# Decay exponents in float32r, and ungrouped projections as one 512-column product with the parts added at eviction

## The chip, the cores and the metric

The kernel runs on one core of a Trainium2 chip. The metric is the time of one execution on the device, in microseconds (us); 2571.78 us is the median of three runs of the kernel before. TensorE multiplies, VectorE, ScalarE and GpSimd do element-wise work, and SyncE's queue issues all the transfers that this text speaks of. PEld is TensorE's loading of weights.

## The reference

Two layers of a decoder trunk of width 2048 over 256 positions. Each layer has eight gated DeltaNet heads and sixteen query heads of sliding-window attention side by side, then a SwiGLU feed-forward part; both halves are modulated by six vectors that come from c.

```
h      = rms_norm(x) * (1 + scale) + shift
qkv, z, b, a, aq, ak, av = split(h @ w_in)        # the projections
q, k, v = silu(causal_conv4(qkv))                  # 4 taps, per channel
g      = -exp(a_log) * softplus(a + dt_bias);  beta = sigmoid(b)
gc     = cumsum(g) in chunks of 64
decay  = exp(where(causal, gc[c] - gc[s], -inf))
lower  = strict(beta * k k^T * decay) + 1;  t_inv = inverse(lower)
o      = delta rule with t_inv, decay, q, k, v;  o = norm(o) * silu(z)
x     += gate * ([o, attention] @ w_out);  x += gate * swiglu(rms_norm(x) ...)
```

## The kernel before

All values are transposed: 128 channels on the partitions, 256 positions along the free side. An activation tile `act` of h holds two halves side by side, the rounded value in float32r (hi) and the rest (lo), 128x512 together. A weight tile is split the same way by ScalarE (`wh`) and VectorE or GpSimd (`wl`). A *block* is the product of one 128x128 weight tile with one activation tile, summed into PSUM over the 16 tiles of h. `mm3` does it as three products of 256 columns (wh with hi, wh with lo, wl with hi) into one 256-column sum. `mm2` does it as two: wh with both halves at once (512 columns, two sums side by side) and wl with hi (256 columns, onto the first). `gemm` uses `mm3`; `gemm_two` and `gemm_pair` use `mm2`. In the feed-forward part all products are `mm2`.

`JOBS` lists the projections of a layer: `ak`, `av`, `aq` for attention, and `k`, `q`, `v`, `z` per DeltaNet head. `project` starts one and hands its PSUM sum `pm` to the work behind it: `conv_silu` (four taps: one ScalarE operation and three VectorE multiply-adds, all reading `pm`), `gate` (z), `attention` or `kv_heads` (rope). In layer 0 the projections that `EARLY` names are computed in groups while h is still coming in, their parts kept in SBUF and added by `added`. `gemm_quad` does the first four of layer 1. The rest, 14 in layer 0 (v of heads 2 to 7 and all z) and 38 in layer 1, are whole projections of 16 blocks, here called ungrouped.

`scores` forms, per head, the decay exponents: GpSimd multiplies the triangular mask `tri` by g (a w3 buffer), three float32 products with the lower mask `ls` and with ones turn that into sums over stretches of g (`qe`), and ScalarE takes the exponential. With it and the products of k and q, VectorE builds the matrix `B` and the small matrices for the inverse. After four heads, `inverses` inverts their chunks in a batch: eight small transfers (`carry`, L126 in the profile: `qi<-mc`) bring the 16x16 blocks to a shape on which VectorE works, eight more bring the result back (`uc<-ui`), and then masks `U`, transposes with `con` (an identity), and a chain of small products of `W`, `U`, `y`, `yn` and `V` follow. `delta` runs the recurrence of one head. A `v` projection of head h waits in `project`'s loop until the delta rule of head h-2 has got to its middle, and that waits for the inverses: two waits per layer, one per batch. In the rest of this text they are the first and the second inverse of a layer.

Modulation vectors are computed beside all that: tiles `wada` of the modulation matrix, each multiplied with `cs` on TensorE or (`CUSTOM_DVE_ANT_0`, `ISA` in the order of instructions) on VectorE.

The order on each engine is fixed when the kernel is built: `Steps` keeps the pending pieces of work and places one when its engine's planned clock allows, by the prices of `Timed` (a fixed and a per-element part per engine) and a constant of 300 ns from one step to the next; `Weights` places loads (six units ahead, four buffers) and splits. So another operation, or another buffer, changes where later ones are put. On the chip each engine runs its own list in order. All instructions are recorded on line 172.

Of the kernel before, what the change touches and what calls it, by code (L numbers as in the profile page):

```python
# [20 lines left out]
F32 = mybir.dt.float32  # L21
F32R = mybir.dt.float32r
AF = mybir.ActivationFunctionType
ALU = mybir.AluOpType
PSUM = bass.MemoryType.PSUM

D, T, L, H, NH, FT = 2048, 256, 2, 8, 16, 44
# [37 lines left out]

CONST = Cols()
for _n, _w in (
    ("ident", 128), ("triX", 256), ("sel", 8), ("ls", 128), ("amask", 256), ("cos", 256), ("sin", 256),
    ("own", 128), ("id16", 16), ("bm", 8), ("m16", 8),
):  # L70
    CONST.add(_n, _w)
PAR = Cols()
# [25 lines left out]
P_, D_, A_, G_, N_ = "tensor", "vector", "scalar", "gpsimd", None  # L98
# [86 lines left out]
JOIN = 4, 2  # L185


HEADS = {"pm": 3, "psm": 5}, {"w3": 5, "B": 6, "z": 3, "dn": 2, "ry": 2}
FFN = {"pr": 2, "psm": 4}, {"mid": NMID}

START = HEADS[0], {"ry": 1, "wx": 8}

STAGE_TOO = {"ak", "vT", "U", "W", "V", "dy", "av", "junk", "yn", "qi", "ui", "uc", "mc", "hi", "y16", "wy"}


class Build:
# [237 lines left out]
def trunk(tc, xT, bada, c, c_col, par, con, w_in, w_ba, w_ada0, w_ada, w_out, w_gu, w_dn, out):  # L434
    nc = Timed(tc.nc)
    with (
# [3 lines left out]
        b = Build(nc, sb, tc)  # L440
        b.lay(START)
        S = Steps(nc)
        pr = b.t("par", [128, PAR.n])
        cn = b.t("con", [128, CONST.n])
        x = b.t("x", [128, KT, T])
        cs = b.t("cs", [128, D])
        cc = b.t("cc", [128, KT])
        mod = b.t("mod", [128, L, 96])
        def wide(a):
            return CONST.at[a][0]  # L450

        nc.dma(cc, c_col)
        nc.gpsimd.memset(cs[:, 0 : KT * 32 + 32], 0.0)
        nc.dma(mod, bada)
        nc.dma(pr, par)
        nc.dma(cn[:, : wide("ls")], con[:, : wide("ls")])
        x_at = [nc.dma(x[:, lo : lo + 4, :], xT[:, lo : lo + 4, :]) for lo in range(0, KT, 4)]

        def P(name, lo=0, hi=None):
# [3 lines left out]
        def C(name):  # L463
            a, n = CONST.at[name]
            return cn[:, a : a + n]

        ident, triX, ls = C("ident"), C("triX"), C("ls")
        tri, ones = triX[:, 0:128], triX[:, 128:256]
        one = ones[:, 0:1]
        half_c = b.t("halfc", [128, 2, 2])  # L470
        nc.vector.memset(half_c[:, 0, :], 0.5)
# [2 lines left out]
        W = Weights(b)  # L474
# [221 lines left out]
        def pump():  # L696
            while first:
                kind, n = first[0]
                if kind == 0 and ada.room():
                    ada.load()  # L700
                elif kind == 1 and W.room():
                    W.load(n)
                elif kind == 2 and b.free["kq"]:
                    load_ba(0)
                    nc.dma(cn[:, wide("ls") :], con[:, wide("ls") :])
                else:
                    break
                first.pop(0)
            u = W.unit()
            if not first:  # L710
                W.load(u + W.AHEAD + 1)
                ada.loads(u)
            W.split(W.p + W.SPLIT, force=False)
# [25 lines left out]
        def gemm(acts, lo=0, hi=None, tag="pm"):  # L739

            S.grab(b, tag)
            q = b.bank(tag)[:, 0:T]
            into(q, mm3, acts, lo, len(acts) if hi is None else hi)
            return Held(q, lambda: b.give(tag))

        def gemm_two(acts, lo=0, hi=None, tag="pm"):

            S.grab(b, tag)
            q = b.bank(tag)
            into(q, mm2, acts, lo, len(acts) if hi is None else hi)  # L750
            return Held(q, lambda: b.give(tag))
# [233 lines left out]
        def added(q, i, then):  # L985
# [3 lines left out]
            q.drop()  # L989
            yield from then(Held(to, lambda: drop_partial(i)))  # L990

        def betas(l, hs, got):
            while None in hs:
                yield N_
            ws = w_of[l]
            yield from b.take("psm", P_)
            q = b.bank()
            for k in range(KT):
                at = slice(k % 4 * 32, k % 4 * 32 + 32)
                nc.tensor.matmul(  # L1000
                    q[at, :], ws[:, k, :], hs[k].rearrange("p a c -> p (a c)").bitcast(F32), start=k < 4, stop=k >= KT - 4
                )
            b.give("kq")
            yield from b.take("cv", A_)
            w = b.t("cv", [128, T])
            nc.scalar.copy(out=w, in_=q[:, 0:T])
            yield D_
            nc.vector.tensor_tensor(out=w, in0=w, in1=q[:, T:], op=ALU.add)
            b.give("psm")
            yield from b.take("psm", P_)  # L1010
            q = b.bank()
            for tb in range(2):
                nc.tensor.matmul(
                    q[:, tb * 16 : tb * 16 + 16], w[:, tb * 128 : tb * 128 + 128], C("id16"), start=True, stop=True
                )
            b.give("cv")
            yield D_
            ba = b.t("ba", [128, 2, 16], bufs=1)
            nc.vector.tensor_copy(out=ba.rearrange("p a c -> p (a c)"), in_=q[:, 0:32])
            b.give("psm")  # L1020
            yield A_
            beta = b.t("beta", [128, 2, 8], bufs=2)
            nc.scalar.activation(out=beta, in_=ba[:, :, 0:8], func=AF.Tanh, scale=0.5)
            na = b.t("nega", [128, 8], bufs=1)
            nc.scalar.activation(out=na, in_=P(f"a_log{l}"), func=AF.Exp)

            v, u, s, s2, y = (b.t(n, [128, 2, 8], bufs=1) for n in ("sp_v", "sp_u", "sp_s", "sp_s2", "sp_y"))
            yield D_
            for tb in range(2):
                nc.vector.tensor_tensor(out=v[:, tb, :], in0=ba[:, tb, 8:16], in1=P(f"dt{l}"), op=ALU.add)  # L1030
            nc.vector.scalar_tensor_tensor(out=u, in0=v, scalar=-1.0, in1=v, op0=ALU.mult, op1=ALU.max)
            yield A_
            nc.scalar.activation(out=u, in_=u, func=AF.Exp, scale=-1.0)
            yield D_
            nc.vector.tensor_scalar(out=beta, in0=beta, scalar1=0.5, scalar2=0.5, op0=ALU.mult, op1=ALU.add)
            nc.vector.tensor_scalar(out=na, in0=na, scalar1=-1.0, scalar2=None, op0=ALU.mult)
            yield D_
            nc.vector.tensor_scalar(out=s, in0=u, scalar1=2.0, scalar2=None, op0=ALU.add)
            nc.vector.reciprocal(out=s, in_=s)
            nc.vector.tensor_tensor(out=s, in0=s, in1=u, op=ALU.mult)  # L1040
            nc.vector.tensor_tensor(out=s2, in0=s, in1=s, op=ALU.mult)
            nc.vector.tensor_scalar(out=y, in0=s2, scalar1=2.0 / 15, scalar2=2.0 / 13, op0=ALU.mult, op1=ALU.add)
            for n in (11, 9, 7, 5, 3, 1):
                nc.vector.tensor_tensor(out=y, in0=y, in1=s2, op=ALU.mult)
                nc.vector.tensor_scalar(out=y, in0=y, scalar1=2.0 / n, scalar2=None, op0=ALU.add)
                if n in (9, 5):
                    yield D_
            nc.vector.tensor_tensor(out=y, in0=y, in1=s, op=ALU.mult)
            g = b.t("g", [128, 2, 8], bufs=2)
            nc.vector.scalar_tensor_tensor(out=g, in0=v, scalar=0.0, in1=y, op0=ALU.max, op1=ALU.add)  # L1050
            for tb in range(2):
                nc.vector.tensor_tensor(out=g[:, tb, :], in0=g[:, tb, :], in1=na, op=ALU.mult)
            got += [beta, g]

        def rope(q, res):
            yield from b.take("cv", N_)
# [165 lines left out]
        def scores(l, h, st, bt):  # L1222

            while len(st["bg"]) < 2:
                yield N_
            beta, g = st["bg"]
            yield from b.take("w3", G_)
            gt = b.t("w3", [128, 384])
            nc.gpsimd.tensor_tensor(out=gt[:, 0:256], in0=triX, in1=g[:, 0, h : h + 1].to_broadcast([128, 256]), op=ALU.mult)
            nc.gpsimd.tensor_tensor(out=gt[:, 256:384], in0=tri, in1=g[:, 1, h : h + 1].to_broadcast([128, 128]), op=ALU.mult)  # L1230
            yield from b.take("psm", P_)
            qe = b.bank()
            nc.tensor.matmul(qe[:, 0:256], ls, gt[:, 0:256], start=True, stop=False)
            nc.tensor.matmul(qe[:, 128:256], ones, gt[:, 256:384], start=False, stop=True)
            nc.tensor.matmul(qe[:, 256:384], ls, gt[:, 256:384], start=True, stop=True)
            b.give("w3")
            yield from b.take("w3", A_)
            E = b.t("w3", [128, 384])
            nc.scalar.activation(out=E, in_=qe[:, 0:384], func=AF.Exp)
# [16 lines left out]
            g1, g2 = b.bank(), b.bank()  # L1256
# [18 lines left out]
            B = b.t("B", [128, 2, 384])  # L1275
# [317 lines left out]
        for l in range(L):  # L1593
# [7 lines left out]
            def project(kind, h, then, rank=1):  # L1601
                if (kind, h) in four:
                    S.add(then(four[kind, h]), rank)
                elif l == 0 and (kind, h) in EARLY:
                    i = TILES.index((kind, h))
                    S.add(added(gemm(hs, *GROUPS[-1]), i, then), rank)
                else:
                    S.add(then(gemm(hs)), rank)

            def put(q):  # L1610
                kvq.append(q)
# [133 lines left out]
```

## Time and profile before

| | |
|---|---|
| median of three runs | 2571.78 us (2567.96 to 2573.69) |
| the profiled execution | 2571.36 us |
| its span, first to last instruction | 2569.6 us |
| mean granted TensorE clock | 0.980 |
| TensorE busy | 2462.8 us, 96% |
| VectorE, ScalarE, GpSimd busy | 1854.1, 1294.3, 432.7 us |
| read from memory | 603.44 MB, 236 GB/s over the span |

The program's stages lie in the span like this: start and first norm to about 180 us, heads of layer 0 to about 550, its output projection and feed-forward part to about 1375, heads of layer 1 to about 1700, its output projection and feed-forward part to the end. A row of the groups gives engine, operation, output<-inputs, shapes, count, then total busy time and the mean duration of one in ns, then idle time before them and what ended it. A row of the timeline gives start, length, engine, line, operation, with idle time before it and its releaser in brackets.

### The profile page before, as it was taken

How to read it: one execution, taken by the hardware profiler on the slowest of the kernel's cores; microseconds unless marked ns; L12 is line 12 of the kernel's file. 1: busy time of each engine (PE TensorE's matmuls, PEld its weight loads, DVE VectorE, ACT ScalarE, POOL GpSimd, SP SyncE). 2: the span in 40 equal slices, each digit the busy share in tenths (PEclk: the TensorE clock that was granted, in tenths of full speed). 3: DMA queues.
4: the chain of work that ended last, by engine and by line, in shares of the span. 5: the costliest groups of instructions: out<-in, count | busy, mean ns of one | idle time of the engine just before them, and what ended most of it. 6: DMA issues, size and time to landing. Idle time of an engine off the chain costs nothing.

```text
span 2569.6 us, 46036 instructions
## 1 busy us (share of the span) xinstructions
PE 2462.8 (96%) x16878; PEld 2174.5 (85%) x16878; DVE 1854.1 (72%) x3823; ACT 1294.3 (50%) x2760; POOL 432.7 (17%) x389
## 2 busy tenths in 40 slices
PE   6999898988999999999999999899899999999998
PEld 4887786987888888888888899899788888888887
DVE  3758767787667999999987876655877655555665
ACT  4346553535545445555445655454555544555553
POOL 1433232670000000000004333246000000000000
PEclk9999998998999999999999999899999999999999
DMA  9987575776777999999984443346677766555564
GB/s 353 338 302 255 194 244 181 249 272 199 244 245 268 341 354 347 352 345 344 328 299 132 133 131 126 118 161 225 214 253 246 243 187 191 189 183 195 180 185 137
DMA packets 192789, 609.08 MB, mean 237 GB/s; under 512 B 27825, under 2 KB 39217, under 8 KB 192561
## 3 DMA queue, kind: packets, MB, share of 16 engines
q1 hardware_dynamic: 192562, 606.14, 68.9%
q8 instruction: 132, 2.16, 0.3%
q14 instruction: 95, 0.78, 0.1%
HBM read 603.44 MB, written 2.10 MB: 236 GB/s over the span
## 4 chain that ended last, share of the span: by engine, by line
PE 52%; issue 32%; DVE 9%; DMA 3%; ACT 2%; POOL 1%; SPq 1%; DVEq 0%; POOLq 0%; ACTq 0%
PE psm L172 19%; PE pr L172 18%; PE pm L172 15%; DMA wada<-w_ada 3%; DVE wl L172 2%; ACT wh L172 1%; DVE wada L172 1%; POOL wl L172 1%; DVE act L172 1%; DVE cv L172 1%; DVE R L172 1%; DVE x L172 1%; DMA wx<-w_ada 0%; SPq L121 0%; DVE ry L172 0%
## 5 line engine op out<-in xcount | busy, mean ns | idle before, releaser
L172 ACT CAST wh<-w 128x512 fp32r<-128x512 f32 x1532 | 894.2, 604 | 456.7 <-PE psm L172 177.0
L172 DVE TENSOR_TENSOR wl<-w,wh 128x512 fp32r<-128x512 f32 (+1 forms) x1293 | 860.3, 683 | 243.7 <-ACT wh L172 234.4
L172 PE MATMUL pr<-act,wh 128*128 128x512 f32 x2816 | 994.7, 395 | 7.3 <-DVE kq L172 4.0
L172 PE MATMUL pr<-act,wl 128*128 128x256 f32 x2816 | 799.0, 284 | 0.0
L172 PE MATMUL pm<-act,wh 128*128 128x256 f32 x3328 | 641.4, 292 | 14.0 <-DVE x L172 4.1
L172 PEld LDWEIGHTS pr<-act,wh 128*128 128x128 f32 x2816 | 531.7, 189 | 132.3 <-DVE act L172 4.7
L172 PEld LDWEIGHTS pm<-act,wh 128*128 128x128 f32 x3328 | 519.0, 192 | 36.3 <-issue 21.2
L172 PEld LDWEIGHTS pr<-act,wl 128*128 128x128 f32 x2816 | 532.2, 189 | 0.0
L172 POOL TENSOR_TENSOR wl<-w,wh 128x512 fp32r<-128x512 f32 (+1 forms) x239 | 331.0, 1395 | 1190.9 <-PE psm L172 762.5
L172 PE MATMUL pm<-act,wl 128*128 128x256 f32 x1664 | 473.3, 284 | 1.4 <-POOL wl L172 1.4
L172 DVE CUSTOM_DVE_ANT_0 wada<-wada,cs 128x1024 f32<-128x1024 f32 x256 | 331.8, 1296 | 129.0 <-DMA wada<-w_ada 128.8
L172 PE MATMUL psm<-act,wh 128*128 128x512 f32 (+1 forms) x1280 | 390.8, 362 | 2.4 <-DVE act L172 2.1
L172 PEld LDWEIGHTS pm<-act,wl 128*128 128x128 f32 x1664 | 318.6, 191 | 2.3 <-POOL wl L172 2.2
L172 PE MATMUL psm<-act,wl 128*128 128x256 f32 x1088 | 308.3, 283 | 0.0
L172 PEld LDWEIGHTS psm<-act,wh 128*128 128x128 f32 x1280 | 228.3, 189 | 46.0 <-issue 6.1
L172 PEld LDWEIGHTS psm<-act,wl 128*128 128x128 f32 x1088 | 205.2, 189 | 0.0
L172 PE MATMUL psm<-mid,wh 128*128 128x512 f32 x512 | 183.4, 396 | 0.0
L172 PE MATMUL psm<-mid,wl 128*128 128x256 f32 x512 | 144.1, 281 | 0.0
L172 POOL TENSOR_TENSOR n2r<-ms,halfc 128x2 f32<-128x2 f32 x5 | 3.5, 690 | 803.5 <-DVE ms L172 803.5
L172 ACT COPY kq<-pr 128x512 f32<-128x512 f32 x88 | 51.6, 587 | 169.3 <-PE pr L172 169.1
L172 PEld LDWEIGHTS psm<-mid,wh 128*128 128x128 f32 x512 | 96.1, 188 | 22.8
L172 DVE TENSOR_TENSOR kq<-pr,kq 128x512 f32<-128x512 f32 x88 | 60.5, 687 | 72.9 <-ACT kq L172 72.9
(188 smaller groups left out, 1957.9 us busy)
## 6 DMA issues: line engine op xcount, KB each, us to landing
w<-w_gu SPq DMA_DIRECT2D x352, 512.0 KB
wada<-w_ada SPq DMA_DIRECT2D x320, 512.0 KB
w<-w_in SPq DMA_DIRECT2D x130, 512.0 KB
w<-w_dn SPq DMA_DIRECT2D x128, 512.0 KB
wx<-w_ada SPq DMA_DIRECT2D x64, 512.0 KB
w<-w_out SPq DMA_DIRECT2D x64, 512.0 KB
w<-w_dn SPq DMA_DIRECT2D x64, 384.0 KB
w<-w_in SPq DMA_DIRECT2D x28, 384.0 KB
```

Of the source, the lines that this page charges most:

```text
L172: return f(*a, **k)
```

## The change

*Projections.* The ungrouped projections run through `gemm_two` instead of `gemm`: `mm2` blocks in a 512-column bank. A new step `whole` takes the sum to SBUF: ScalarE copies the second half into a `pq` tile (two buffers), VectorE adds the first half onto it, the bank is given back, and the work behind reads the `pq` tile where it read PSUM.

*Decay exponents.* `betas` splits g into a rounded float32r part and its rest (`g2`). In `scores` one GpSimd operation multiplies `ls` by both parts for both halves of the positions (`lg`, 128x512, one buffer of its own), and six float32r products with the mask `triR` (or with g itself spread over the columns) replace three in float32. `triR` is rounded once at the start by a ScalarE copy from a tile `tri0`, which has its own transfer ahead of those of x; the same values as ones serve the other sums.

*Buffers.* w3 goes from five to four, B from six to five.

```
 HEADS = ... {"w3": 5, "B": 6, ...}   ->   {"w3": 4, "B": 5, ..., "pq": 2}

+tri0 = b.t("tri0", [128, 256], bufs=1)
+tri_at = nc.dma(tri0, con[:, wide("triX") :])
 x_at = [nc.dma(x[:, lo : lo + 4, :], xT[:, lo : lo + 4, :]) for lo in range(0, KT, 4)]
...
+triR = b.t("triR", [128, 256], F32R)
+nc.scalar.copy(out=triR, in_=tri0)
+ones = triR[:, 128:256].bitcast(F32)
...
+def whole(q, then):
+    yield from b.take("pq", A_)
+    to = b.t("pq", [128, T])
+    nc.scalar.copy(out=to, in_=q.ap[:, T:])
+    yield D_
+    nc.vector.tensor_tensor(out=to, in0=q.ap[:, 0:T], in1=to, op=ALU.add)
+    q.drop()
+    yield from then(Held(to, lambda: b.give("pq")))
...
 betas:
+g2 = b.t("g2", [128, 2, 2, 8], F32R, bufs=1)
+nc.vector.tensor_copy(out=g2[:, :, 0, :], in_=g)
+nc.vector.tensor_tensor(out=g2[:, :, 1, :], in0=g, in1=g2[:, :, 0, :].bitcast(F32), op=ALU.subtract)
...
 scores:
-gt = b.t("w3", [128, 384])
-nc.gpsimd.tensor_tensor(out=gt[:, 0:256], in0=triX, in1=g[:, 0, h : h + 1].to_broadcast([128, 256]), op=ALU.mult)
-nc.gpsimd.tensor_tensor(out=gt[:, 256:384], in0=tri, in1=g[:, 1, h : h + 1].to_broadcast([128, 128]), op=ALU.mult)
+lg = b.t("lg", [128, 2, 2, 128], F32R, bufs=1)
+nc.gpsimd.tensor_tensor(out=lg..., in0=ls (four times), in1=g2 of head h (spread over 128 columns), op=ALU.mult)
...
-nc.tensor.matmul(qe[:, 0:256], ls, gt[:, 0:256], start=True, stop=False)
-nc.tensor.matmul(qe[:, 128:256], ones, gt[:, 256:384], start=False, stop=True)
-nc.tensor.matmul(qe[:, 256:384], ls, gt[:, 256:384], start=True, stop=True)
+for i in range(2):
+    nc.tensor.matmul(qe[:, 0:256], lg[:, 0, i, :], triR, start=i == 0, stop=False)
+    nc.tensor.matmul(qe[:, 128:256], g2[:, 1, i, h : h + 1].to_broadcast([128, 128]), triR[:, 0:128], start=False, stop=i == 1)
+for i in range(2):
+    nc.tensor.matmul(qe[:, 256:384], lg[:, 1, i, :], triR[:, 0:128], start=i == 0, stop=i == 1)
...
 project:
-    S.add(then(gemm(hs)), rank)
+    S.add(whole(gemm_two(hs), then), rank)
```

The planner puts other operations elsewhere in the two stages of the heads; in the feed-forward stages the order stays. Two places follow.

VectorE before the second inverse of layer 1 (U: the masks with which the inverse's last part starts; wada, n: a modulation tile and its sum; y: the inverse's next step; z, vT: ends of a z and a v projection). Before:

```order
L172 TENSOR_TENSOR wl_20266<-w_20054,wh_20265 128x512
L172 SCALAR_TENSOR_TENSOR vT_20093<-th_20274,cv_20211 128x256
L172 TENSOR_TENSOR wl_20289<-w_20109,wh_20288 128x512
L172 SCALAR_TENSOR_TENSOR z_20301<-th_20302,pm_20201 128x256
L172 TENSOR_TENSOR U_20305<-uc_20225,con_67 128x128 x2
L172 TENSOR_TENSOR U_20308<-uc_20225,con_67 128x128 x2
L172 ISA wada_20286,n_3695_16484<-wada_20286,cs_69 128x1024
L172 ISA n_3695_16484 128x1
L172 TENSOR_TENSOR y_3671_16390<-psm_20322,con_67 128x8x16
```

and after:

```order
L172 SCALAR_TENSOR_TENSOR cv_19677<-pq_19627,par_66,cv_19677 128x253
L172 TENSOR_TENSOR pq_19713<-pm_19616,pq_19713 128x256
L172 SCALAR_TENSOR_TENSOR vT_19522<-th_19715,cv_19677 128x256
L172 SCALAR_TENSOR_TENSOR z_19719<-th_19720,pq_19713 128x256
L172 ISA wada_19699,n_3712_16318<-wada_19699,cs_69 128x1024
L172 ISA n_3712_16318 128x1
L172 TENSOR_TENSOR U_19724<-uc_19659,con_67 128x128 x2
L172 TENSOR_TENSOR U_19727<-uc_19659,con_67 128x128 x2
L172 TENSOR_TENSOR y_3688_16231<-psm_19741,con_67 128x8x16
```

The modulation tile has moved ahead of the masks, and the addition of the z projection's parts (pq) stands among the last operations. On SyncE's queue there, before:

```order
L126 DMA qi_19936<-mc_18168 8x16x16 x8
L121 DMA w_19955<-w_in 128x1024
L121 DMA w_20007<-w_in 128x1024
L121 DMA w_20054<-w_in 128x1024
L121 DMA w_20109<-w_in 128x1024
L121 DMA w_20163<-w_in 128x1024
L121 DMA w_20223<-w_in 128x1024
L126 DMA uc_20225<-ui_16394 128x1x16 x8
L121 DMA w_20272<-w_in 128x1024
L121 DMA wada_20286<-w_ada 128x1024
```

and after:

```order
L126 DMA qi_19412<-mc_17850 8x16x16 x8
L121 DMA w_19446<-w_in 128x1024
L121 DMA w_19489<-w_in 128x1024
L121 DMA w_19540<-w_in 128x1024
L121 DMA w_19588<-w_in 128x1024
L121 DMA w_19631<-w_in 128x1024
L126 DMA uc_19659<-ui_16235 128x1x16 x8
L121 DMA w_19689<-w_in 128x1024
L121 DMA wada_19699<-w_ada 128x1024
```

One weight load of six that stood between the two sets of carries is gone.

TensorE before the first inverse of layer 0 (con,U: transposes of the masks; W,B and y,U: the products behind them; pm: a projection). Before:

```order
L172 MATMUL psm_3912<-con_67,U_3890 128x128 x2
L172 MATMUL pm_3829<-act_2187,wh_3682 128x256 x2
L172 MATMUL pm_3829<-act_2187,wl_3683 128x256
L172 MATMUL psm_3925<-con_67,U_3893 128x128 x2
L172 MATMUL pm_3924<-act_1645,wh_3719 128x256 x2
L172 MATMUL pm_3924<-act_1645,wl_3720 128x256
L172 MATMUL psm_3934<-W_3928,B_2904 128x64 x2
L172 MATMUL pm_3924<-act_1683,wh_3719 128x256 x2
L172 MATMUL pm_3924<-act_1683,wl_3720 128x256
```

and after:

```order
L172 MATMUL pm_3862<-act_2191,wh_3760 128x256 x2
L172 MATMUL pm_3862<-act_2191,wl_3761 128x256
L172 MATMUL psm_3930<-ak_2338,ry_3554 128x128
L172 MATMUL psm_3931<-ak_2338,ry_3554 128x128
L172 MATMUL psm_3930<-ak_2338,ry_3554 128x256
L172 MATMUL psm_3931<-ak_2338,ry_3554 128x256
L172 MATMUL psm_3949<-con_67,U_3936 128x128 x2
L172 MATMUL psm_3952<-con_67,U_3939 128x128 x2
L172 MATMUL psm_3964<-W_3955,B_2885 128x64 x2
L172 MATMUL psm_115<-wada_3786,cs_69 32x256 x4
```

The transposes and first products stood among blocks of a projection; now they follow the last block before the wait and an attention head's products.

More of the change, by code (lines that the diff above doesn't have):

```diff
@@ L67 @@
 for _n, _w in (
-    ("ident", 128), ("triX", 256), ("sel", 8), ("ls", 128), ("amask", 256), ("cos", 256), ("sin", 256),
-    ("own", 128), ("id16", 16), ("bm", 8), ("m16", 8),
+    ("ident", 128), ("sel", 8), ("ls", 128), ("amask", 256), ("cos", 256), ("sin", 256),
+    ("own", 128), ("id16", 16), ("bm", 8), ("m16", 8), ("triX", 256),
 ):
@@ L185 @@
 JOIN = 4, 2
-HEADS = {"pm": 3, "psm": 5}, {"w3": 5, "B": 6, "z": 3, "dn": 2, "ry": 2}
+HEADS = {"pm": 3, "psm": 5}, {"w3": 4, "B": 5, "z": 3, "dn": 2, "ry": 2, "pq": 2}
 FFN = {"pr": 2, "psm": 4}, {"mid": NMID}
 START = HEADS[0], {"ry": 1, "wx": 8}
-STAGE_TOO = {"ak", "vT", "U", "W", "V", "dy", "av", "junk", "yn", "qi", "ui", "uc", "mc", "hi", "y16", "wy"}
+STAGE_TOO = {"ak", "vT", "U", "W", "V", "dy", "av", "junk", "yn", "qi", "ui", "uc", "mc", "hi", "y16", "wy", "lg", "tri0"}
 class Build:
@@ L442, in trunk, with wide @@
         S = Steps(nc)
+        def wide(a):
+            return CONST.at[a][0]
         pr = b.t("par", [128, PAR.n])
-        cn = b.t("con", [128, CONST.n])
+        cn = b.t("con", [128, wide("triX")])
         x = b.t("x", [128, KT, T])
@@ L448, in trunk @@
         mod = b.t("mod", [128, L, 96])
-        def wide(a):
-            return CONST.at[a][0]
         nc.dma(cc, c_col)
@@ L465, in C @@
             return cn[:, a : a + n]
-        ident, triX, ls = C("ident"), C("triX"), C("ls")
-        tri, ones = triX[:, 0:128], triX[:, 128:256]
+        ident, ls = C("ident"), C("ls")
+        triR = b.t("triR", [128, 256], F32R)
+        nc.floor = tri_at
+        nc.scalar.copy(out=triR, in_=tri0)
+        nc.floor = 0
+        ones = triR[:, 128:256].bitcast(F32)
         one = ones[:, 0:1]
@@ L704, in pump @@
                     load_ba(0)
-                    nc.dma(cn[:, wide("ls") :], con[:, wide("ls") :])
+                    nc.dma(cn[:, wide("ls") :], con[:, wide("ls") : wide("triX")])
                 else:
@@ L1052, in betas @@
                 nc.vector.tensor_tensor(out=g[:, tb, :], in0=g[:, tb, :], in1=na, op=ALU.mult)
-            got += [beta, g]
+            g2 = b.t("g2", [128, 2, 2, 8], F32R, bufs=1)
+            nc.vector.tensor_copy(out=g2[:, :, 0, :], in_=g)
+            nc.vector.tensor_tensor(out=g2[:, :, 1, :], in0=g, in1=g2[:, :, 0, :].bitcast(F32), op=ALU.subtract)
+            got += [beta, g2]
         def rope(q, res):
@@ L1225, in scores @@
                 yield N_
-            beta, g = st["bg"]
-            yield from b.take("w3", G_)
-            gt = b.t("w3", [128, 384])
-            nc.gpsimd.tensor_tensor(out=gt[:, 0:256], in0=triX, in1=g[:, 0, h : h + 1].to_broadcast([128, 256]), op=ALU.mult)
-            nc.gpsimd.tensor_tensor(out=gt[:, 256:384], in0=tri, in1=g[:, 1, h : h + 1].to_broadcast([128, 128]), op=ALU.mult)
+            beta, g2 = st["bg"]
+            yield G_
+            lg = b.t("lg", [128, 2, 2, 128], F32R, bufs=1)
+            nc.gpsimd.tensor_tensor(
+                out=lg.rearrange("p a b c -> p (a b) c"), in0=ls.unsqueeze(1).to_broadcast([128, 4, 128]),
+                in1=g2[:, :, :, h].bitcast(F32).rearrange("p a b -> p (a b)").unsqueeze(2).to_broadcast([128, 4, 128]),
+                op=ALU.mult,
+            )
             yield from b.take("psm", P_)
             qe = b.bank()
-            nc.tensor.matmul(qe[:, 0:256], ls, gt[:, 0:256], start=True, stop=False)
-            nc.tensor.matmul(qe[:, 128:256], ones, gt[:, 256:384], start=False, stop=True)
-            nc.tensor.matmul(qe[:, 256:384], ls, gt[:, 256:384], start=True, stop=True)
-            b.give("w3")
+            for i in range(2):
+                nc.tensor.matmul(qe[:, 0:256], lg[:, 0, i, :], triR, start=i == 0, stop=False)
+                nc.tensor.matmul(
+                    qe[:, 128:256], g2[:, 1, i, h : h + 1].to_broadcast([128, 128]), triR[:, 0:128], start=False, stop=i == 1
+                )
+            for i in range(2):
+                nc.tensor.matmul(qe[:, 256:384], lg[:, 1, i, :], triR[:, 0:128], start=i == 0, stop=i == 1)
             yield from b.take("w3", A_)
```

## The prediction

> **What bounds the kernel now.** I read the page first: busy times, the line of granted clocks, and the chain that ended last.
>
> ```profile
> PE 2462.8 (96%) x16878; PEld 2174.5 (85%) x16878; DVE 1854.1 (72%) x3823; ACT 1294.3 (50%) x2760; POOL 432.7 (17%) x389
> PEclk9999998998999999999999999899999999999999
> PE 52%; issue 32%; DVE 9%; DMA 3%; ACT 2%; POOL 1%; SPq 1%; DVEq 0%; POOLq 0%; ACTq 0%
> ```
>
> TensorE is busy 96% of the span, and over half of the chain is its own work; of VectorE's 1854 us the chain holds 9%. So a saving on TensorE counts nearly whole, except in the stages where it waits. For these I took busy times by 50 us slices over the two stages that the change touches: the layer-0 heads (180 to 550 us) and the layer-1 heads (1375 to 1700 us). Columns: stretch, length, busy time of PE, PEld, DVE, ACT, POOL, granted clock, DMA share, GB/s.
>
> ```profile
> 250.00:300.00 50.00, 45.30 (x418) 36.41 (x417) 42.79 (x123) 29.15 (x83) 16.15 (x20) 1.00 0.71 238
> 300.00:350.00 50.00, 46.89 (x463) 38.29 (x461) 32.16 (x100) 29.66 (x90) 14.37 (x15) 0.97 0.55 184
> 400.00:450.00 50.00, 41.62 (x306) 35.11 (x305) 35.65 (x91) 19.03 (x53) 8.31 (x7) 0.80 0.52 178
> 1350.00:1400.00 50.00, 45.58 (x360) 41.23 (x360) 39.82 (x87) 26.94 (x60) 23.33 (x22) 0.97 0.42 137
> 1400.00:1450.00 50.00, 48.03 (x382) 44.11 (x381) 38.88 (x110) 34.88 (x95) 20.44 (x28) 1.00 0.38 127
> 1450.00:1500.00 50.00, 48.80 (x408) 46.18 (x407) 42.76 (x103) 27.73 (x67) 19.17 (x18) 1.00 0.44 140
> 1500.00:1550.00 50.00, 47.97 (x428) 44.90 (x427) 32.98 (x85) 29.09 (x83) 16.12 (x17) 1.00 0.35 117
> 1650.00:1700.00 50.00, 40.63 (x368) 37.84 (x368) 22.08 (x70) 17.29 (x55) 11.17 (x9) 0.80 0.30 100
> ```
>
> TensorE still leads, with 1 to 5 us idle per slice. The exceptions are the slices at 400 and 1650: 8 to 9 us idle and a clock of 0.80, which is 20 us at half speed if the rest ran at full. Those are the second inverse of each layer, where the next v projection waits for a delta rule.
>
> The profiled execution took 2571.36 us (span 2569.6), 0.4 below the median of 2571.78; I carry differences over to the median.
>
> **A. Projections as two products instead of three.** 52 projections (14 in layer 0, 38 in layer 1) of 16 weight tiles, 832 blocks in all. The price of both forms stands in stages that run nothing else: 1720 to 1795 us is the output projection of layer 1 in the old form, 2215 to 2415 us a down projection, already in the new one.
>
> ```profile
> 1720.00:1795.00 75.00, 75.00 (x634) 75.00 (x633) 38.08 (x62) 34.96 (x64) 54.71 (x40) 1.00 0.68 226
> 2215.00:2415.00 200.00, 200.00 (x1141) 175.27 (x1140) 118.46 (x197) 106.24 (x196) 0.00 (x0) 1.00 0.56 187
> ```
>
> Old: 634/3 = 211.3 blocks in 75 us, 354.9 ns each. New: 1141/2 = 570.5 blocks in 200 us, 350.6 ns. The number of columns streamed is the same (768), so dropping 832 products of 16,878 buys only 4.3 ns a block: 832 x 4.3 = **-3.6 us**. The bounds: 0 if the idle slots of the heads' stages swallow it, -4.2 with a 5 ns difference. I take -3.6, because TensorE is the releaser in most of these slices. What is won after a stage's last wait on a delta rule is won whole; what is won before it can be lost.
>
> **B. Decay exponents.** One head in the trace (start, length, operation; lengths overlap, so starts count):
>
> ```profile
> 1431.25 0.49 PE L172 MATMUL psm<-con,w 128*128 128x128 f32 x3
> 1431.49 0.49 PE L172 MATMUL pm<-act,wh 128*128 128x256 f32 x2
> 1431.82 0.28 PE L172 MATMUL pm<-act,wl 128*128 128x256 f32 x1
> 1431.94 1.04 PE L172 MATMUL psm<-w,con 128*128 128x256 f32 x6
> 1432.73 0.49 PE L172 MATMUL pm<-act,wh 128*128 128x256 f32 x2
> 1433.05 0.29 PE L172 MATMUL pm<-act,wl 128*128 128x256 f32 x1
> ```
>
> The three float32 products (six records) hold TensorE from 1431.94 to 1432.73, 0.79 us. The two projection products behind them take 0.32 instead of 2 x 0.118 (354.9/3), 0.08 more, as they do behind any float32 product. That is 0.87 us a head. After: two 256-column float32r products at 0.118 and four of 128 columns, of which the trace shows none. Lower end: by column, 350.6/768 = 0.457 ns, 0.058 each. Upper end: two passes, as float32 makes them, 0.215 each. I take 0.105, the step between records in the first row, (0.49 - 0.28)/2, since it has the same weight tile and the same 128 columns. So 2 x 0.118 + 4 x 0.105 = 0.66, or 0.21 less a head: 16 x 0.21 = **-3.4 us**; ends 16 x (0.236 + 0.232 - 0.87) = -6.4 and 16 x (0.236 + 0.86 - 0.87) = +3.6.
>
> [...]
>
> GpSimd's two products per head become one of 512 columns, for which I have its split of a weight tile. (Columns of the groups: count, busy us, mean ns, idle before.)
>
> ```profile
> L172 POOL TENSOR_TENSOR wl<-w,wh 128x512 fp32r<-128x512 f32 x226 | 320.7, 1429 | 1155.7 <-PE psm L172 755.2 <-ACT wh L172 341.6 <-PE pm L172 24.7
> L172 POOL TENSOR_TENSOR w<-con,g 128x256 f32<-128x256 f32 x16 | 11.7, 734 | 9.3 <-DVE g L172 9.1 <-DVE qn L172 0.2
> L172 POOL TENSOR_TENSOR w<-con,g 128x128 f32<-128x128 f32 x16 | 9.4, 586 | 0.0
> L172 ACT COPY act<-pm 128x256 f32<-128x256 f32 x8 | 3.0, 374 | 3.2 <-PE pm L172 3.1
> L172 DVE TENSOR_TENSOR act<-pm,act 128x256 f32<-128x256 f32 x64 | 26.2, 417 | 10.8 <-PE pm L172 10.6
> L172 DVE SCALAR_TENSOR_TENSOR cv<-pm,par,cv 128x255 f32<-128x255 f32 x30 | 14.3, 476 | 6.0 <-ACT cv L172 6.0
> L172 DVE SCALAR_TENSOR_TENSOR cv<-act,par,cv 128x255 f32<-128x255 f32 x18 | 12.1, 672 | 0.0
> L172 DVE SCALAR_TENSOR_TENSOR cv<-act,par,cv 128x254 f32<-128x254 f32 x18 | 10.5, 582 | 0.0
> L172 DVE SCALAR_TENSOR_TENSOR cv<-act,par,cv 128x253 f32<-128x253 f32 x18 | 9.4, 522 | 0.1
> ```
>
> 734 + 586 = 1320 ns against 1429: no change that matters on an engine at 17%. The two small operations that split g lie once per layer on VectorE, far ahead of the heads: nothing. Of the five w3 buffers one served this product, which now has its own (lg); B's fifth is free when the delta rule of head 2 ends, which stands 30 blocks ahead of the place where head 7 needs it: nothing either.
>
> **G. Load on the other engines.** Each of the 52 tiles gains a ScalarE copy (374 ns: 19 us in all, at 50% busy, taken at nothing) and a VectorE add (417 ns: 21.7 us). Thirty of them are convolutions that now read SBUF where they read PSUM. The three multiply-adds cost 672 + 582 + 522 = 1776 ns there, against 3 x 476 = 1428: 0.35 us more, 10.5 us in all. VectorE gets 32 us, of which layer 1 bears 38 x 0.417 + 24 x 0.35 = 24.2. At 1450 to 1500 us it has 7.2 us free per slice and gains 24.2/7 = 3.5. Does TensorE then wait? Within layer 1 it idles no more in the slices with 39 to 43 us of VectorE (1400, 1450) than in one with 33 (1500): slope nil. In layer 0, 10.6 us more VectorE goes with 1.6 less TensorE (250 against 300), 0.15 per us: 24.2 x 0.15 = 3.6. I take **+1**, nearer to layer 1's own rows; ends 0 and +3.6.
>
> [...]
>
> **D. The last wait of layer 1** (around 1650 us). First three pieces of the chain of waits, then SyncE, VectorE and TensorE there:
>
> ```profile
> 1646.12 1.34 DVE wl L172
> 1647.53 0.33 SPq L121
> 1647.90 0.67 SPq L126
> ```
>
> ```profile
> 1647.90 5.26 SPq L126 DMA_DIRECT2D uc<-ui  x8
> 1653.28 0.39 SPq L121 DMA_DIRECT2D w<-w_in  x1
> 1653.71 0.43 SPq L121 DMA_DIRECT2D wada<-w_ada  x1
> ```
>
> ```profile
> 1651.40 0.90 DVE L172 TENSOR_TENSOR U<-uc,con 128x128 f32<-128x128 f32 x4 [0.24 <-DMA uc<-ui]
> 1658.86 1.23 DVE L172 CUSTOM_DVE_ANT_0 wada<-wada,cs 128x1024 f32<-128x1024 f32 x1 [6.56 <-DMA wada<-w_ada]
> ```
>
> ```profile
> 1651.75 0.94 PE L172 MATMUL psm<-con,U 128*128 128x128 f32 x4 [1.98 <-DVE U L172]
> 1652.74 1.23 PE L172 MATMUL psm<-W,B 128*128 128x64 f32 x8
> 1660.35 0.69 PE L172 MATMUL psm<-y,U 128*128 128x64 f32 x2 [6.38 <-DVE y L172]
> ```
>
> A modulation tile (wada) is in VectorE's queue ahead of y. Its transfer is issued at 1653.71, behind the eight small carries, and VectorE stands 6.56 us for it. The masks U, their transposes and the first products W,B are done meanwhile, between 1651.40 and 1653.97. In the changed order the wada operation stands ahead of the U masks, so these 2.57 us follow the landing. To that comes that the last k and q products lie four blocks later (4 x 0.35 = 1.4). Against it, one weight load fewer stands ahead of the carries on SyncE: they wait in that queue until 1647.90 for a load that itself waits for the wl of 1646.12, the operation after the last one on ui; of these 1.8 us I take 1.5 as won. I take 2.57 + 1.4 - 1.5 = **+2.5**; ends +1.1 (2.57 - 1.5) and +4.0 (2.57 + 1.4).
>
> **C. The inverses of layer 0.**
>
> ```profile
> 292.59 0.64 PE L172 MATMUL psm<-wada,cs 128*32 128x256 f32 x8 [2.48 <-DMA wada<-w_ada]
> ```
>
> Before the first inverse of layer 0, the transposes of U and the products up to y,U ran among the last seven blocks before the wait; now they all follow the last block. That uncovers 7 x 0.355 = 2.5 us, and up to 1.8 more as the last k and q products of the batch lie five blocks later. The wait for wada just ahead, 2.48 us, then falls into a time in which only the chain is late, and can vanish. I take 2.5 - 2.48 = **0**, ends -2.5 and +4.3. The second inverse of layer 0 keeps its order.
>
> **F. Start.** One more issue on SyncE ahead of x, at the 0.39 us of such a row: **+0.4**, ends 0 and +1 (ScalarE's first work waits for that tile).
>
> Sum: -3.6 - 3.4 + 1 + 2.5 + 0 + 0.4 = **-3.1 us**, on the median 2568.7, say **2569**.
>
> **The rivals.**
> *Clearly faster.* 128 columns cost 0.058 and the last wait of layer 1 does not grow, because the wada transfer is issued early: -3.6 - 6.4 + 0.4 + 1 = -8.6, 2563; with the 2.48 of layer 0 gone too, 2561. For it: weight loads have room in the new form (PEld 175 of 200). Against it: nothing in this trace runs 128 columns below 0.1.
> *VectorE becomes the bound in layer 1.* In the three slices with 38.9 to 42.8 us of VectorE every added microsecond would go on the path: 3 x 3.5 = 10.4 instead of 1, so -3.1 - 1 + 10.4 = +6.3, 2578. It decides from where a weight split (wl) or a k,q product comes late more than once per head. For it: three engines now hand a projection on one after the other, with two pq buffers. Against it: 7 us free per slice.
> *Inverses longer and at half clock.* C and D at their upper ends (+4.3, +4.0) add 5.8; the clock stays low for some 7 us more, costing half: +3.5 more. -3.1 + 9.3 = +6.2, 2578.
> *128 columns take two passes.* B is +3.6: -3.1 + 3.4 + 3.6 = +3.9, 2576.
> *The blocks gain nothing.* A is 0: +0.5, 2572.
>
> **How the numbers follow.** What this kernel's timing can tell from no change is about 0.2%, 5.1 us: below 2566.6 is faster, above 2576.9 slower. The forecast has 0.42, its own range 2563 to 2575 (A, B, D, G at their likelier ends); of that 0.32 is within 0.2%, 0.07 faster, 0.03 slower. Clearly faster 0.26. VectorE the bound 0.13; long inverses 0.06 (0.01 within); two passes 0.05 (half within); no block gain 0.08 (within). Together: faster 0.33, same 0.43, slower 0.24. The range 2558 to 2580 leaves out a tenth on each side: the faster case with every term at its end (-4.2 - 6.4 - 2.5), and the slower ones in pairs.
>
> **What would show it.** A: stretches of layer-1 projections at 350 to 351 ns a block; wrong if 355. B: from the first lg product to the projection product behind the last one about 0.66 us; 0.47 or 1.1 for the ends. G: TensorE's idle by slice in 1400 to 1600 within 1 us of before, and few waits on wl, kq or pq. D: behind the wada operation VectorE's four U masks, and TensorE's idle there near 9 us instead of 6.38. C: the stretch around 290 to 314 us as long as before. I am wrong above all if 128 columns cost far from 0.105, or if the waits before the inverses move by more than 4 us.

## The result, and the profile after

The changed kernel takes 2583.7 us (median of four runs, 2581.1 to 2584.15), the kernel before 2572.28 in the same comparison: ratio 1.004, 95% interval 1.0023 to 1.0058. It is **11.4 us slower**. I had predicted 2569 within 2558 to 2580, 3 us faster.

The page of the changed kernel, the lines that answer to the first three shown of before:

```profile
span 2582.4 us, 44467 instructions
...
PE 2466.7 (96%) x16046; PEld 2134.2 (83%) x16046; DVE 1891.8 (73%) x3868; ACT 1316.7 (51%) x2813; POOL 450.7 (17%) x384
...
PEclk9999898999999999999999999899999999999999
```

There are 832 TensorE instructions fewer (16,046 against 16,878), and TensorE is busy 3.9 us *more*, although the blocks and the exponents take less (below). The heads of layer 0 ran at a lower clock (0.94 against 0.96, below), which I take for the reason; no run separates it. Its idle time grew by 8.9 (2582.4 - 2466.7 against 2569.6 - 2462.8). VectorE has 37.7 us more.

To place the loss I cut both traces at the same two pairs of weight blocks, before the heads of each layer and in or just before the output projection (block 320 to 832, and 3040 to 3750). Columns: stretch, length, then busy time of PE, PEld, DVE, ACT, POOL, clock, DMA share, GB/s. The kernel before:

```profile
197.98:539.88 341.90, 317.78 (x2819) 271.56 (x2817) 259.63 (x670) 177.68 (x490) 148.99 (x135) 0.96 0.67 227
1348.01:1723.35 375.34, 354.05 (x2985) 331.20 (x2985) 263.88 (x665) 212.12 (x558) 138.88 (x138) 0.97 0.39 129
```

The changed kernel:

```profile
196.54:547.56 351.02, 322.43 (x2594) 262.91 (x2593) 269.80 (x684) 182.41 (x504) 154.25 (x129) 0.94 0.64 222
1351.64:1735.77 384.13, 354.29 (x2377) 299.84 (x2377) 288.65 (x696) 225.42 (x596) 152.37 (x139) 0.96 0.36 126
```

Layer 0 is 9.1 us longer, layer 1 8.8 us. In layer 1 TensorE's busy time is the same (354.3 against 354.1) and the whole loss is idle time, 29.8 instead of 21.3 us. In layer 0 busy time grows by 4.7 and idle time by 4.5, at a lower clock (0.94 against 0.96). What lies outside the two stretches is 5.1 us shorter in this pair of executions. I don't explain that part: the piece between the two stretches, mostly feed-forward, is 4.0 us shorter here and moves between that and 1.9 us longer among the kernels below that keep the planner's constant at 300.

The exponents of one head, as TensorE does them now (start, length, operation):

```profile
261.10 0.28 PE L172 MATMUL psm<-triR,lg 128*128 128x256 f32 x1
261.22 0.22 PE L172 MATMUL psm<-triR,g 128*128 128x128 f32 x1
261.27 0.33 PE L172 MATMUL psm<-triR,lg 128*128 128x256 f32 x1
261.44 0.22 PE L172 MATMUL psm<-triR,g 128*128 128x128 f32 x1
261.50 0.39 PE L172 MATMUL psm<-triR,lg 128*128 128x128 f32 x2
261.72 0.45 PE L172 MATMUL pm<-act,wh 128*128 128x256 f32 x2
```

From 261.10 to 261.72 it is 0.62 us where it was 0.79. This is one of the shortest: except for the first head, the heads take 0.62 to 0.74 (0.79 to 0.90 before), and all 16 together 2.2 us less.

The place before the last inverse, SyncE, VectorE and TensorE:

```profile
1642.22 13.70 SPq L121 DMA_DIRECT2D w<-w_in  x5
1657.31 5.28 SPq L126 DMA_DIRECT2D uc<-ui  x8
1662.69 0.39 SPq L121 DMA_DIRECT2D w<-w_in  x1
1663.13 0.43 SPq L121 DMA_DIRECT2D wada<-w_ada  x1
```

```profile
1668.14 1.22 DVE L172 CUSTOM_DVE_ANT_0 wada<-wada,cs 128x1024 f32<-128x1024 f32 x1 [4.41 <-DMA wada<-w_ada]
1669.29 0.08 DVE L172 DVE_READ_ACCUMULATOR2_ANT n<- 128x1 f32 x1
1669.29 0.89 DVE L172 TENSOR_TENSOR U<-uc,con 128x128 f32<-128x128 f32 x4
```

```profile
1669.63 1.12 PE L172 MATMUL psm<-con,U 128*128 128x128 f32 x4 [9.74 <-DVE U L172]
```

The masks U stand behind the modulation tile, as the order said; TensorE waits 9.74 us in one piece where it waited 1.98 and 6.38.

### The profile page after: what moved, and what is told of

Same layout as the page of the kernel before. It is cut to its first block, busy times and chain, and to the rows that moved or that the text cites. A ratio compares the mean times of both kernels' runs of the same rounds, so it can differ in the third digit from the quotient of the medians.

```text
span 2582.4 us, 44467 instructions
## 1 busy us (share of the span) xinstructions
PE 2466.7 (96%) x16046; PEld 2134.2 (83%) x16046; DVE 1891.8 (73%) x3868; ACT 1316.7 (51%) x2813; POOL 450.7 (17%) x384
## 5 line engine op out<-in xcount | busy, mean ns | idle before, releaser
L172 PE MATMUL pm<-act,wh 128*128 128x256 f32 (+1 forms) x2496 | 637.4, 333 | 15.6 <-DVE x L172 4.6
L172 POOL TENSOR_TENSOR wl<-w,wh 128x512 fp32r<-128x512 f32 (+1 forms) x250 | 349.5, 1406 | 1202.2 <-ACT wh L172 1119.5
L172 PEld LDWEIGHTS pm<-act,wh 128*128 128x128 f32 x2496 | 420.4, 192 | 69.3 <-issue 22.3
L172 PEld LDWEIGHTS psm<-mid,wh 128*128 128x128 f32 x512 | 96.2, 188 | 22.5
```

What stands on the lines that cost most here:

```text
L172: return f(*a, **k)
```

## The experiments

The ratio is that of each kernel to the kernel before, run with it on the same chip. Theory 1: the eviction of the projections costs the loss. Theory 2: the loss lies in the order that the planner makes when any operation changes. Theory 3: the exponents and their buffers cost it.

**The parts by themselves.** e1 has the exponents alone, e2 the projections alone, e3 the whole change without the eviction, e4 the eviction without the two-product blocks.

```
e1: -S.add(whole(gemm_two(hs), then), rank)     +S.add(then(gemm(hs)), rank)
e2: kernel before, +whole, +S.add(whole(gemm_two(hs), then), rank), "B": 5, "pq": 2
e3: +S.add(then(Held(q.ap[:, 0:T], q.drop)), rank)  with q = gemm_two(hs)
e4: +S.add(whole(gemm(hs), then), rank), copy and add of the 256 columns
```

> Exponents alone: projections are three products read from PSUM as before; w3 4, B 5, lg, tri0 as in the changed kernel. Theory 1 (the loss comes from the step that evicts a projection: one ScalarE copy, one VectorE add, and slower reads from SBUF): 2 to 4 us faster than before, by the 0.17 us per head that the changed kernel's trace shows. Theory 2 (the loss is where the planner's new order happens to put the inverses' chains): anything from -4 to +6. Theory 3 (the exponents and their buffers cost it): 6 to 10 us slower.

> Projections alone: two products and the eviction step, exponents in float32 as before; w3 5, B 5, pq 2. Theory 1: 12 to 16 us slower than before, the changed kernel's loss and the exponents' gain on top. Theory 2: anything from 0 to +12. Theory 3: no change or 2 us faster.

> The changed kernel without the eviction step: the work behind a projection reads the first half of the 512-column bank from PSUM, so the second half (wh with lo) is computed and left out of the result. Theory 1: 4 to 7 us faster than before (the blocks' 1.7 to 3.6 and the exponents' 2.7). Theory 2: from -7 to +5, as its order is new too. Theory 3: 6 us slower, as the changed kernel.

> The changed kernel with three products per block again and an eviction step of the same two operations (ScalarE copies the 256-column sum to pq, VectorE adds the sum once more: the projections come out doubled). Theory 1: as slow as the changed kernel, +11 to +15 against before. Theory 2: from 0 to +14. Theory 3: +8 to +12, like the changed kernel.

| | median, us | before | ratio (95%) |
|---|---|---|---|
| e1 exponents | 2576.79 | 2572.75 | 1.0014 (1.0002 to 1.0027) |
| e2 projections | 2577.67 | 2572.75 | 1.0015 (1.0004 to 1.0026) |
| e3 no eviction | 2586.83 | 2572.75 | 1.0051 (1.0035 to 1.0067) |
| e4 eviction, three products | 2588.63 | 2572.75 | 1.0065 (1.0046 to 1.0085) |

e3 loses as much as the changed kernel without the step that I then suspected most. So theory 1 falls as the sole cause, and by e1 and e2 theory 3 does too. e1 is not faster although most heads' exponents are.

**The order alone.** e5 takes only the smaller buffers into the kernel before, e6 only another planner constant; e7 and e8 are the changed kernel in two more orders.

```
e5: kernel before, "w3": 5 -> 4, "B": 6 -> 5
e6, e8: HOP = 300 -> 350 (kernel before, changed kernel)      e7: HOP = 300 -> 250 (changed kernel)
```

> The kernel before with the smaller buffer counts of the changed one alone (w3 four instead of five, B five instead of six), nothing else; the planner places the work anew. After the first four runs I hold theory 2 (the loss is where the planner's new order puts the inverses' chains and what they wait for) above theory 1 (the eviction step), since the kernel without that step lost as much. Theory 2: +2 to +7 against before, most of it around the first inverse of layer 0 and the second inverse of layer 1. Theory 4 (buffers matter only by real waits for a free one, of which I saw none): within 1.5 us.

> The kernel before, operation for operation, with the planner's constant from one step to the next at 350 instead of 300 ns: only the order on the engines differs. Theory 2: the kernel before holds an order that fits its waits, and another costs +3 to +12. Rival (the order hardly matters, the operations do): within 2 us of before.

> The changed kernel with the planner's constant at 250 instead of 300 ns: the same operations in another order. Theory 2: anywhere from -4 to +16 against before, and over 3 us away from the changed kernel's +11. Rival (the operations cost it): +9 to +13.

> The changed kernel with the planner's constant at 350 instead of 300 ns: the same operations in a third order. Theory 2: anywhere from -4 to +16 against before, and apart from the other two orders by over 3 us. Rival: +9 to +13.

Measured: e5 2569.5 us (ratio 0.9992, 0.9981 to 1.0003: no change that can be told); **e6 2588.86 us, 1.0063 (1.0045 to 1.0081), 16 us slower with the same operations in another order** (the planner also gave three of some 1570 weight splits to GpSimd instead of VectorE, and two copies to ScalarE); e7 2585.55, 1.0052 (1.0033 to 1.0071); e8 2587.83, 1.0063 (1.0046 to 1.0080), against 2572.65 of before. My expectation for e5 was a miss. e7 and e8 came out within 4 us of the changed kernel, where theory 2 would have had them spread; the rival's +9 to +13 holds for e7 and misses e8 by 2. The two stretches of e6:

```profile
203.22:556.77 353.55, 322.36 (x2794) 276.06 (x2792) 262.73 (x660) 177.34 (x488) 144.60 (x134) 0.94 0.63 215
1367.01:1740.52 373.51, 353.03 (x2986) 330.36 (x2985) 261.83 (x660) 212.43 (x558) 144.99 (x143) 0.97 0.39 130
```

Layer 0 is 11.7 us longer than before (353.55 against 341.90) with nearly the same work (25 of its 2819 products now lie outside it), layer 1 isn't. The first stretch also begins 5.2 us later.

**The operations in a held order.** Here the planner is told the old prices, counts no eviction and holds a projection's bank as long as before. TensorE, ScalarE, VectorE and SyncE then keep e5's order, with the new operations put in where the work behind begins. e9 both parts, e10 the exponents, e11 the projections with their eviction, e12 the projections without it.

```
+nc.charge("tensor", "matmul", (q[:, 0:T], w, a), {})   three times a block, then the two products uncounted
+nc.scalar.real.copy(out=to, in_=q.ap[:, T:])           eviction uncounted
+nc.vector.real.tensor_tensor(out=to, in0=q.ap[:, 0:T], in1=to, op=ALU.add)
```

> Both parts of the change, but planned at the old prices: the planner counts three products per block, the old exponents and no eviction, and a projection's PSUM bank counts as held until the work behind has read its tile. So TensorE, ScalarE, VectorE and SyncE keep the order of the kernel with the smaller buffers alone (e5, -3 us), with the new operations put in. Theory 2 (the changed kernel lost by its new order): -2 to -8 against before, that is -4 to +1 against e5. Theory 1 (its operations cost it): +5 to +12 against before.

> The exponents alone, in e5's order by the same means. Theory 2: 2 to 3 us faster than e5 (16 heads at 0.17 us), -4 to -6 against before. Theory 3 (the exponents cost it): slower than e5 by 4 or more.

> The projections alone (two products and the eviction), in e5's order. Theory 2: -3 to +3 against e5: the blocks win 1.7 to 3.6, the eviction's longer way from product to k, q and v costs 1 to 4. Theory 1: +8 or more against e5.

> As e11 without the eviction: two products per block, the work behind reads the first half of the bank from PSUM, and the second half (wh with lo) is left out of the result. In e5's order. My term A alone: 3.6 us faster than e5, or 1.7 if products between blocks take the gain back, as the changed kernel's trace has it; the difference to e11 is the eviction's price on the path (my term G, +1).

| | median, us | before | ratio (95%) |
|---|---|---|---|
| e9 both | 2601.94 | 2570.3 | 1.0116 (1.0097 to 1.0135) |
| e10 exponents | 2565.42 | 2570.3 | 0.9982 (0.9969 to 0.9995) |
| e11 projections | 2600.08 | 2570.3 | 1.0108 (1.0091 to 1.0126) |
| e12 projections, no eviction | 2561.89 | 2570.3 | 0.9962 (0.9947 to 0.9977) |

With the order held, the blocks' saving arrives, clear of e5, and the eviction alone turns -8 into +30. The exponents' saving arrives against the kernel before; against e5 it isn't clear of noise. The groups show how the eviction costs this. (Group rows as before; e11 first, where these operations have lines of their own, then the changed kernel.)

```profile
L1013 DVE TENSOR_TENSOR pq<-pm,pq 128x256 f32<-128x256 f32 x52 | 21.8, 420 | 33.0 <-ACT pq L1012 32.8
```

```profile
L172 DVE TENSOR_TENSOR pq<-pm,pq 128x256 f32<-128x256 f32 x52 | 21.6, 415 | 2.1 <-ACT pq L172 1.9
L172 ACT COPY pq<-pm 128x256 f32<-128x256 f32 x52 | 19.3, 372 | 42.4 <-PE pm L172 38.1 <-DVE cv L172 4.0
L172 DVE SCALAR_TENSOR_TENSOR cv<-pq,par,cv 128x254 f32<-128x254 f32 x30 | 22.9, 763 | 0.3
L172 DVE SCALAR_TENSOR_TENSOR cv<-pq,par,cv 128x255 f32<-128x255 f32 x30 | 19.9, 662 | 1.0 <-ACT cv L172 0.8
L172 DVE SCALAR_TENSOR_TENSOR cv<-pq,par,cv 128x253 f32<-128x253 f32 x30 | 18.9, 629 | 0.4
```

In e11, in the old order, VectorE stands 33 us in its queue for ScalarE's copies, and what is behind the add there waits with it. e11's stretch of layer 1 is 400.99 us long, with 41.0 idle. In the changed kernel the planner puts the add later, so it waits 2.1 us, and the work behind the projection comes later instead. My expectations for e9 and e11 were far off: I had counted the eviction's way but not the queue in which it would stand.

**How wide the orders spread.** e13 and e14 are the kernel before at the constants 250 and 325; e15 and e16 the change without eviction at 250 and 350.

> The kernel before, operation for operation, with the planner's constant at 250 instead of 300 ns. If its order at 300 is a good one among many (theory 2), any other costs: +3 to +16. If 350 was merely a bad one: within 3 us of before.

> The kernel before with the constant at 325 ns. Theory 2: +3 to +16. If 350 was merely a bad one: within 3 us of before.

> The changed kernel without the eviction step (the second half of each projection's bank is computed and left out of the result), at 250 ns; it stands against the changed kernel at 250 (+13). If the order alone makes the loss: +8 to +16. If the eviction costs by itself: -5 to +5.

> The changed kernel without the eviction step (the second half of each projection's bank is computed and left out of the result), at 350 ns; it stands against the changed kernel at 350 (+15). If the order alone makes the loss: +8 to +18. If the eviction costs by itself: -5 to +5.

| | median, us | before | ratio (95%) |
|---|---|---|---|
| e13 before, 250 | 2578.6 | 2573.55 | 1.0025 (1.0015 to 1.0036) |
| e14 before, 325 | 2583.12 | 2573.55 | 1.0034 (1.0021 to 1.0047) |
| e15 no eviction, 250 | 2588.34 | 2573.55 | 1.0052 (1.0033 to 1.0072) |
| e16 no eviction, 350 | 2572.64 | 2573.55 | 0.9998 (0.9988 to 1.0009) |

So the same operations of the kernel before cost 0, +5, +10 or +16 us by the order that the planner makes. Not all of it lies in the heads. At the other constants the first stretch begins 5 to 9 us later (197.98 before; 203.22 in e6, 205.06 in e13, 207.17 in e14), where the changed kernel, planned at 300, lost nothing (196.54). The two stretches together are 9.8 us longer in e6, 11.1 in e13 and 0.4 in e14. The change without eviction stands at +14, +15 and -1 at 300, 250 and 350, the changed kernel at +11, +13 and +15. e15 came out as the order alone would have it, e16 as the eviction would. e8 against e16, at an equal constant, says that the eviction costs 16; the changed kernel against e3 says -3, e7 against e15 -2. By whole times the eviction's price can't be told from the order's.

Layer 1 alone tells it. There I took TensorE's idle time (length less PE busy) of the stretch 3040 to 3750 in all kernels that the planner placed with an eviction, and in all without:

| | idle in layer 1, us |
|---|---|
| with eviction | changed 29.8, e2 26.8, e4 25.7, e7 27.2, e8 29.2: mean 27.7 |
| without | before 21.3, e1 19.4, e3 26.7, e5 20.8, e6 20.5, e10 22.5, e12 19.9, e13 23.2, e14 21.7, e15 23.9, e16 22.1: mean 22.0 |

Of these the row of e16, and of e12, the fastest:

```profile
1351.25:1722.27 371.02, 348.94 (x2378) 297.71 (x2377) 265.51 (x666) 212.55 (x558) 138.97 (x131) 0.96 0.38 131
```

```profile
1340.30:1713.25 372.95, 353.08 (x2377) 299.60 (x2377) 263.84 (x665) 211.65 (x558) 137.60 (x138) 0.96 0.37 130
```

Ten of the eleven without lie below all five with (the exception is e3, 26.7). Each figure is of one execution; those of e3, e14 and e15 are of the longest of their runs. Four pairs differ by the eviction and the order that follows from it, with the constant and the other operations equal. For these, TensorE's idle time in layer 1, and the part of it that stands ahead of the products of k and q:

| with, without | idle in layer 1, us | of it ahead of `psm<-kq` |
|---|---|---|
| changed, e3 | 29.8, 26.7 | 4.2, 1.1 |
| e7, e15 | 27.2, 23.9 | 5.5, 0.0 |
| e8, e16 | 29.2, 22.1 | 9.2, 1.3 |
| e4, e1 | 25.7, 19.4 | 2.2, 0.0 |

So the eviction costs 3 to 7 us in layer 1, 5 on average, and nearly all of it (4.7 on average) is waiting for k and q. In layer 0, where it has 14 of its 52 tiles, the five lengths with it are 343 to 354 us, the eleven without 336 to 357: no difference beyond the order's spread.

**The best version** that computes the whole result is e10, the float32r exponents in a held order: 2565.42 us, ratio 0.9982 (0.9969 to 0.9995), faster than both kernels. (e12 is faster still, but leaves out a part of every ungrouped projection.) Against e5, whose order it has, that is 2.6 us by the two ratios, whose intervals overlap.

## Why the prediction was wrong, step by step

- **A, blocks (-3.6): the price right, the gain not where the sum had it.** In layer 1, rows of six or more blocks with no other product between them take 350.7 ns a block in the changed kernel and 356.2 in the kernel before. e12 against e5, the same order: layer 0 335.99 against 341.16, layer 1 372.95 against 373.96, -6.2 in all. But it does not fall by the number of blocks: layer 0 has 224 of them and gets 5.2, layer 1 has 608 and gets 1.0. Part of layer 0's gain must be a shorter wait; I did not separate it.
- **B, exponents (-3.4): the price about right, a wait left out.** The six products take 0.62 to 0.74 us a head, where I expected 0.66, and 2.2 us less over 16 heads. But the first head of each layer now waits longer for `lg`, 2.03 and 2.50 us against 1.55 and 1.27 before: 1.7 us that I had put at nothing. e10 against e5 is -2.6, not clear of noise. The two lg products of 128 columns of float32r take 0.22 us together, 0.11 each, where I had taken 0.105.
- **G, load on VectorE (+1, ends 0 and +3.6): the step that failed first.** It is about 5 us in layer 1 (3 to 7 by the four pairs). The sign that I had set was missed too: TensorE's idle time from 1400 to 1600 us should have stayed within 1 us by slice, and it grew by 1.3, 1.7, 0.9 and 1.7. Of these slices the one of before that isn't shown above, then those of the changed kernel:

```profile
1550.00:1600.00 50.00, 48.74 (x439) 45.25 (x437) 32.40 (x94) 30.24 (x84) 20.35 (x19) 1.00 0.38 129
```

```profile
1400.00:1450.00 50.00, 46.75 (x275) 38.30 (x275) 43.10 (x110) 33.05 (x89) 22.60 (x24) 0.97 0.33 117
1450.00:1500.00 50.00, 47.07 (x287) 39.57 (x286) 43.55 (x99) 31.14 (x79) 21.65 (x20) 1.00 0.40 139
1500.00:1550.00 50.00, 47.06 (x330) 39.18 (x330) 37.10 (x93) 30.74 (x88) 19.03 (x17) 0.97 0.33 117
1550.00:1600.00 50.00, 47.01 (x313) 38.82 (x312) 37.43 (x93) 30.42 (x80) 21.23 (x19) 1.00 0.36 127
```

I priced the extra 24 us by how little TensorE's idle time varied with VectorE's busy share between slices. What counts is not the share (TensorE idles about 3 us in these slices with 43 us of VectorE and with 37) but the way from a projection's last product to k, q and v: it got a copy, an add and slower multiply-adds longer. The wait of TensorE for k and q grew over both layers from 3.1 us to 5.3 (last column; first before, then the changed kernel):

```profile
L172 PE MATMUL psm<-kq 128*128 128x512 f32 x32 | 16.9, 611 | 3.1 <-DVE kq L172 3.1
```

```profile
L172 PE MATMUL psm<-kq 128*128 128x512 f32 x32 | 17.2, 619 | 5.3 <-DVE kq L172 5.2
```

The rival "VectorE becomes the bound" (+6.3 in all) named this place and not the mechanism: no slice above is full.
- **The multiply-adds** were under-priced too: 662 + 763 + 629 = 2054 ns against 1428 from PSUM, where I had taken 1776.
- **C, inverses of layer 0 (0, ends -2.5 and +4.3): wrong.** The wait at the first inverse, from the last block before it to the first behind it (443 to 444), grew from 13.9 to 22.6 us, and the stretch from block 400 to its end by 5.9. It goes with the order, not with the eviction: the same wait is 22.2 us in e3, which has none, 9.3 in e2, which has one, and 4.6 in e5, another order of the old operations. The wait for wada, which I had let vanish, is still there:

```profile
303.27 0.64 PE L172 MATMUL psm<-wada,cs 128*32 128x256 f32 x8 [2.68 <-DMA wada<-w_ada]
```

It now stands inside the chain, ahead of the products on y, and the chain behind it runs at a clock of 0.50. Four us of the chain, first before, then the changed kernel, and the slice that answers to the one of before (46.89 busy, 463 instructions, clock 0.97):

```profile
308.00:312.00 4.00, 3.72 (x32) 2.49 (x28) 2.09 (x10) 0.98 (x4) 0.51 (x1) 0.91 0.00 0
```

```profile
308.00:312.00 4.00, 4.00 (x69) 2.15 (x68) 2.22 (x10) 0.98 (x4) 0.00 (x0) 0.50 0.02 4
300.00:350.00 50.00, 45.23 (x379) 35.76 (x378) 27.52 (x92) 26.03 (x88) 11.94 (x12) 0.83 0.46 160
```

The rival "inverses longer and at half clock" (+6.2 in all) had this place right, though 5.9 lies above its +4.3; D did not reach its end there.

- **D, the last inverse (+2.5): right.** The masks came behind the modulation tile, and the wait, from the last block before it to the first behind it (3647 to 3648), grew from 20.1 to 22.1 us.
- **F (+0.4): can't be told.** The first projection block began 1.6 us earlier in this execution; in kernels without that edit it moves from 1.2 earlier to 0.9 later.
- **The frame failed.** I added terms to the old order and took its ends for the range. No rival said that the order as such, with the same operations, is worth 5 to 16 us over the kernel, and up to 11 in the heads' stretches; e6, e13 and e14 show it. The kernel before sits at the best of the four constants tried. That does not mean that every new order loses: e5 is one and lost nothing, and e16 has two-product blocks at -1.
- **What the sum would have been.** With G at 5, C at 5.9 and the 1.7 us for `lg`, and the other terms as forecast, it comes to +8.5. The rest of the 11.4 is not placed.

What stays open: which single place of a new order costs how much, and whether an order exists in which the eviction's 5 us are hidden. No run here has one made for it.

## What to carry to other kernels

Where a planner writes the order, separate an edit's operations from the order they cause: charge the new operations at the old prices, so that the order stays, and change a constant of the planner without any edit, to learn what the order alone is worth. Here that was up to 16 us against savings of about 3 and 6. And price an extra step behind a product by the length of the chain to the next product that waits for it, not by the engine's busy share; the same two operations cost 2 us or 33 in VectorE's queue by where they stood.

## What the runs showed of the hardware that I had not expected

In the changed kernel a VectorE operation that reads two tiles in SBUF took 1.59 us while GpSimd worked, against 0.48, three times as long (VectorE, then GpSimd):

```profile
1641.69 0.48 DVE L172 SCALAR_TENSOR_TENSOR cv<-pq,par,cv 128x255 f32<-128x255 f32 x1 [0.58 <-ACT cv L172]
...
1643.48 1.59 DVE L172 SCALAR_TENSOR_TENSOR cv<-pq,par,cv 128x254 f32<-128x254 f32 x1
...
1645.80 0.48 DVE L172 SCALAR_TENSOR_TENSOR cv<-pq,par,cv 128x253 f32<-128x253 f32 x1
```

```profile
1642.25 2.55 POOL L172 TENSOR_TENSOR wl<-w,wh 128x512 fp32r<-128x512 f32 x2 [1.75 <-ACT wh L172]
```

The same operation took 0.48 us with GpSimd idle and 1.59 when it started while GpSimd split weight tiles; it ended (1645.07) just behind GpSimd (1644.80). The changed kernel has 90 such multiply-adds on `pq`. The 46 that met no work of GpSimd took 475 ns on average, none over 484; the 44 that did took 904, up to 1592. In the kernel before 90 read PSUM, and the 50 of them that met GpSimd took 475, none over 484. I had priced the operations from rows (`cv<-act`) of which 19 in 54 met GpSimd, not 44 in 90.

In the exponents a float32r product of 128 columns is hardly cheaper than one of 256 in a block, 0.11 us against 0.118. The six products, with six different weight tiles and 1024 columns together, take 0.62 us; at the columns' price of the blocks (350.6 / 768 = 0.457 ns) it would be an estimated 0.47. The last two, of 128 columns each, take 0.22 us together. Whether it is the weight tile that holds them was not tested.
